# Key and value projections of a memory cross-attention: a third pair of k-tiles taken in seven products

## The chip, the cores and the metric

The kernel runs on one core of a Trainium2 chip. The metric is device time in microseconds (us) of one launch; the time of a version is the median of its runs. A core has a matrix engine (TensorE: PE in the profile, with its weight loads as PEld), three engines that work on tiles (VectorE: DVE, ScalarE: ACT, GpSimd: POOL), and a queue from which almost all transfers are issued (SP). Each engine takes its instructions in the order in which the program was built, and waits on semaphores for the results of the others.

## The reference

A streaming-encoder block of one layer over 256 tokens of width 2048, in float32: a gated feed-forward, a mixer, a cross-attention to 256 memory tokens, and a second feed-forward. What matters here is the cross-attention:

```python
def mem_cross_attention(h, mem_h, w_q, w_kv, w_o):
    b, s, _ = h.shape
    q = (h @ w_q).reshape(b, s, XATTN_HEADS, XATTN_HEAD_DIM)
    kv = (mem_h @ w_kv).reshape(b, mem_h.shape[1], 2, XATTN_HEADS, XATTN_HEAD_DIM)
    k, v = kv[:, :, 0], kv[:, :, 1]
    logits = jnp.einsum('bshd,bmhd->bhsm', q, k).astype(jnp.float32) * (XATTN_HEAD_DIM ** -0.5)
    p = jax.nn.softmax(logits, axis=-1).astype(v.dtype)
    o = jnp.einsum('bhsm,bmhd->bshd', p, v).reshape(b, s, D_MODEL)
    return o @ w_o
```

`w_kv` is 2048 x 4096: 16 k-tiles of 128 rows, and four blocks of 1024 columns, which are taken as keys of heads 0 and 1, values of heads 0 and 1, keys of heads 2 and 3, values of heads 2 and 3.

## The kernel before

**Precision by halves.** Every float32 operand is kept as a high and a low part in a faster format, and one product of tiles is three matmuls: high by high, high by low, low by high (`products`, L357). A weight tile arrives by a 1 MB transfer as `raw`; ScalarE casts the high part `wh` (L1579), VectorE subtracts to make the low part `wl` (`low_parts`, L453). `raw`, `wh` and `wl` have three buffers each.

**Units and the stream.** A block multiplies 256 tokens by 1024 columns. It is cut into eight units, one for each pair of k-tiles; the order of the units is a tuple such as `KV_ORDER`. `Stream.emit` (L70) writes the program out unit by unit: the weights of the unit two places ahead are split, the transfer three places further is issued, then the unit's matmuls follow. Side work is put among the units by `st.op(f, after)`. VectorE's and ScalarE's work on weights keeps its written order (`in_turn`, L257). The order of matmuls on TensorE is settled when the program is built, and neighbouring units can be interleaved by it.

**Two kinds of unit.** A plain unit (`unit_p`) is 2 k-tiles x 2 token halves x 2 column halves x 3 = 24 matmuls of 128 x 512. The other kind (`unit_s`, `seven`, L493) takes the 2 x 2 x 2 product of half blocks in seven products instead of eight, which is 7 x 3 = 21 matmuls, after the scheme of Strassen and Winograd. For that, sums of the operands are needed:

- of the weights, for each such unit and block: `split_seven` (L471) makes four sums in `T` with three VectorE instructions (L486), splits three of the raw parts into `xh` (ScalarE, L279) and `xl` (VectorE, L280), and the four sums into `wh` (ScalarE, two casts, L489) and `wl` (VectorE, L453);
- of the tokens, once for each pair of k-tiles: `Sums.make` (L413) makes them on VectorE in a scratch tile `j` and splits them into a tile `ye` and, for one of them, over the second half of the pair's own columns of `xs`, which holds the memory tokens here.

Partial results of the seven products lie in two extra PSUM tiles (`parts`), which `combine` (L570) adds up after the last such unit; `join` (L584) adds the result to the block's other two PSUM tiles. There are four PSUM tiles in all. The logits, the softmax and the products with the values run among the units of the following block, and use PSUM tiles too.

**Where the sums lie.** While the keys and values are made, `T` takes turns with the tile of `combine` in two buffers called `sg`, and `xh` and `xl` have together two buffers called `att`:

```python
    KV_HOMES = {"T": [("sg", D, 2)], "xh": [("att", 3 * NB, 2)], "xl": [("att", 3 * NB, 2)]}
```

So the `xh` and `xl` of one unit fill both, and those of the next unit of this kind go where these have been read for the last time. In the blocks of the queries `xh` and `xl` have other places besides (`Q_HOMES`, L1229).

**The blocks in question.** All four use the order (1, 5, 2, 0, 3, 6, 4, 7), with pairs 0 and 4 in seven products: the fourth and the seventh unit (L1288, L1374 to L1387). The sums of the tokens of these two pairs are made at the start of the first key block.

Of the kernel before, what the change touches and what calls it, by code (L numbers as in the profile page):

```python
# [20 lines left out]
NB = 512  # L21
# [78 lines left out]
def build(ctx, tc, I, out):  # L100
# [89 lines left out]
    xs = main.tile([P, KT, 2, S], F32R, tag="xs", name="xs")  # L190
# [79 lines left out]
    def among_weights(f):  # L270


        scalar, vector = behind_weights(f)
        latest["vector"] = vector
        if scalar is not None:
            latest["scalar"] = scalar
# [349 lines left out]
    def wload(dst, w, k0, n, n0, cols=NB):  # L626
        nc.sync.dma_start(
            dst, w[k0 * P : (k0 + n) * P, n0 : n0 + cols].rearrange("(k p) n -> p k n", p=P)
        )
# [9 lines left out]
    def wwide(w, n0, k0=0, nk=KT):  # L639

        def src(k):
            def load(raw):
                raw = raw.rearrange("p (k n) -> p k n", n=2 * NB)
                if len(loaded) < 3:
                    for kk in range(2):
                        parts = (0, NB) if not loaded else (0,)
                        for c in parts:
                            n = 2 * NB // len(parts)
                            wload(raw[:, kk : kk + 1, c : c + n], w, k + kk, 1, n0 + c, n)
                else:  # L650
                    wload(raw, w, k, 2, n0, 2 * NB)
                next(first_loads, None)
                loaded.append(1)
            return load
        return [src(k0 + k) for k in range(0, nk, 2)]
# [577 lines left out]
    def homes(of):  # L1233
        return lambda: scope.update(shared={tag: list(of[tag]) for tag in of})
# [47 lines left out]
    w_q, w_kv, w_o = I["xattn_w_q"][0], I["xattn_w_kv"][0], I["xattn_w_o"][0]  # L1282
# [2 lines left out]
    q_sums, Q_ORDER = Sums("ye", xs, (4, 5), True, 2), ((0, 1, 2, 3, 6, 4, 5, 7),  # L1285
                                                        (0, 1, 4, 2, 5, 3, 6, 7))
    Q_SEVENS = ((4,), (4, 5))
    kv_sums, KV_ORDER = Sums("ye", xs, (0, 4), True, 2), (1, 5, 2, 0, 3, 6, 4, 7)  # L1288
    held = {}

    def ev_Q(b):
# [10 lines left out]
    def turn_K(h):  # L1302
        v = rows_turned(held["K", h])
        K = xa["K", h] = xt("K", [P, 4, 2, M], F32R, tag="kv", bufs=2)
        split(K[:, :, 0, :], K[:, :, 1, :], v)

    def ev_V(b):
        def evict(j, c):
            V = xa["V", 2 * b + j] = xt("V", [P, 2, 2, XHD], F32R, tag="kv", bufs=2)
            split(V[:, :, 0, :], V[:, :, 1, :], c)  # L1310
        return evict

    def logits(h):
        ps = ptile(uid("pl"))
        for t in range(2):
            tok = slice(t * P, (t + 1) * P)
            parts = [(d, a, b) for d in range(4) for a, b in ((0, 0), (0, 1), (1, 0))]
            for i, (d, a, b) in enumerate(parts):
                nc.tensor.matmul(  # L1319
                    ps[:, t, :M], ys[:, 4 * h + d, a, tok], xa["K", h][:, d, b, :],  # L1320
                    start=i == 0, stop=i == 11,
                )
        scale = XHD ** -0.5
        nm, sm = xt("nm", [P, 2], bufs=2), xt("sm", [P, 2], bufs=2)
        nc.vector.tensor_reduce(out=nm, in_=ps[:, :, :M], axis=AX.X, op=ALU.max)
        nc.vector.tensor_scalar_mul(nm, nm, -scale)
        pr = xa["P", h] = xt("P", [P, 2, M], bufs=2)
        for t in range(2):
            nc.scalar.activation(
                pr[:, t, :], ps[:, t, :M], AF.Exp, scale=scale, bias=nm[:, t : t + 1],  # L1330
                accum_out=sm[:, t : t + 1],
            )
        nc.vector.reciprocal(out=sm, in_=sm)
        for t in range(2):
            nc.vector.tensor_scalar_mul(pr[:, t, :], pr[:, t, :], sm[:, t : t + 1])

    def probs(h):
        ps = ptile(uid("pt"))
        for mtile in range(2):
            for t in range(2):  # L1340
                nc.tensor.transpose(
                    ps[:, mtile, t * P : (t + 1) * P], xa["P", h][:, t, mtile * P : (mtile + 1) * P], ident
                )
        if h % 2 == 0:
            xt("PT", [P, D], F32R)
        PT = xa["PT", h] = xa["PT"][:, h % 2 * 4 * S : (h % 2 + 1) * 4 * S].rearrange(
            "p (m a s) -> p m a s", m=2, a=2
        )
        split(PT[:, :, 0, :], PT[:, :, 1, :], ps[:, :, :S])

    def values(h):
        for p in range(2):
            ps = ptile(uid("pv"))
            for d in range(2):
                col = slice((2 * p + d) * P, (2 * p + d + 1) * P)
                parts = [(m, a, b) for m in range(2) for a, b in ((0, 0), (0, 1), (1, 0))]
                for i, (m, a, b) in enumerate(parts):
                    nc.tensor.matmul(  # L1358
                        ps[:, d, :S], xa["V", h][:, m, a, col], xa["PT", h][:, m, b, :],
                        start=i == 0, stop=i == 5,  # L1360
                    )
            split_pair(ys, 4 * h + 2 * p, ps[:, :, :S])
# [8 lines left out]
            for c, after in enumerate((5, 7, 6, 9)):  # L1371
                st.op(lambda c=c: mem_fold(c), after)
    st.op(homes(KV_HOMES))
    for g, after in zip(kv_sums.pairs, (0, 2)):  # L1374
        st.op(lambda g=g: among_weights(lambda: kv_sums.make(g)), after)
    for b in range(2):
        block_s(wwide(w_kv, b * 2 * NB), xs, kv_sums, KV_ORDER, lambda j, c, b=b: held.__setitem__(
            ("K", 2 * b + j), c))
        for j in (1, 0):
            h = 2 * b + j  # L1380
            st.op(lambda h=h: turn_K(h), 1)
        for h in (2 * b, 2 * b + 1):
            st.op(lambda h=h: logits(h), 2)
            st.op(lambda h=h: probs(h), 3)
        block_s(wwide(w_kv, D + b * 2 * NB), xs, kv_sums, KV_ORDER, ev_V(b))
        for h in (2 * b, 2 * b + 1):
            st.op(lambda h=h: values(h), 1)  # L1387
# [211 lines left out]
def program(shapes):  # L1599
    import concourse.bacc as _bacc  # L1600

    nc = _bacc.Bacc("TRN2", target_bir_lowering=False, num_devices=1)
    args = {
        name: nc.dram_tensor(f"in_{name}", shapes[name], F32, kind="ExternalInput").ap()
        for name in _INS
    }
    out = nc.dram_tensor("out", _OUT, F32, kind="ExternalOutput").ap()
    with tile.TileContext(nc, schedule_with_timeline_sim=True) as tc, ExitStack() as ctx:
        build(ctx, tc, args, out)
    return nc  # L1610
# [10 lines left out]
```

## Time and profile before

| | us |
|---|---|
| median of three runs | 2083.23 (2082.67 to 2083.72) |
| the profiled execution, whole time | 2082.87 |
| the profiled execution, span from the first to the last instruction | 2081.1 |
| between the two | 1.8 |

The granted TensorE clock was 0.999 on average. The key and value blocks lie between about 1085 and 1289 us of the span; their 32 transfers of 1 MB took 5.0 us from issue to landing (median).

How to read the views: the page's first part gives busy time, share of the span and instructions of each engine; its groups give line, engine, operation, the tile written and the tiles read, count, busy time and the mean of one in ns, then the idle time of that engine just before. The timeline gives start and length in us, the instruction (consecutive ones of a kind are merged, with xN), and in square brackets the engine's idle time before it with what ended it. A matmul's length in these views is from its start to its modelled end; matmuls overlap, so the distance from one start to the next is what it takes of TensorE's time.

### The profile page before, as it was taken

Reading aid. Unit: us, or ns where it says so; the run is one execution under the profiler, and the core shown is the slowest. Engines: PE = TensorE matmul, PEld = TensorE weight load, DVE = VectorE, ACT = ScalarE, POOL = GpSimd, SP = SyncE. Lnnn points to the kernel's source line nnn. Section 1 sums busy time; section 2 is a strip of 40 time slices with the busy share of each in tenths; the row PEclk is TensorE's granted clock in tenths of the full one; section 3 lists DMA queues with packets and bytes.
Section 4 is the critical chain, followed back from the end, with each engine's and each line's share of the span. In section 5 each row is a group of like instructions: output and inputs, shape, how many; then the busy total and the mean of one; then the engine's idle time right before and its main releaser. Section 6 shows DMA issues by size and latency. Waiting matters only on the chain.

```text
span 2081.1 us, 24343 instructions
## 1 busy us (share of the span) xinstructions
PE 2069.6 (99%) x9660; PEld 1727.6 (83%) x9660; DVE 1786.6 (86%) x1670; ACT 1138.7 (55%) x1128; POOL 98.4 (5%) x87
## 2 busy tenths in 40 slices
PE   9999999999999999999999999999999999999998
PEld 7888888888888888888888888888888888888886
DVE  7998899989998677679788777879988999889987
ACT  7655455644654545455755444656554555545554
POOL 0000000000000000000000000000100010000001
PEclk9999999999999999999999999999999999999999
DMA  7666666566656755557655455666576665676664
GB/s 264 207 201 227 235 223 219 185 223 239 227 199 218 249 167 182 162 185 272 226 179 190 162 182 180 205 222 203 181 242 212 237 207 193 223 242 222 210 226 151
DMA packets 131178, 435.95 MB, mean 209 GB/s; under 512 B 9844, under 2 KB 13528, under 8 KB 130680
## 3 DMA queue, kind: packets, MB, share of 16 engines
q1 hardware_dynamic: 130888, 433.86, 61.9%
q8 instruction: 76, 1.25, 0.2%
q10 hardware_dynamic: 176, 0.53, 0.1%
q14 instruction: 38, 0.31, 0.0%
HBM read 417.58 MB, written 16.78 MB: 209 GB/s over the span
## 4 chain that ended last, share of the span: by engine, by line
PE 99%; DMA 0%; DVE 0%; ACT 0%; SPq 0%; DVEq 0%; issue 0%; ACTq 0%
PE pt L362 59%; PE pt L507 27%; PE pa L347 7%; PE pb L362 2%; PE ph L780 1%; PE pl L1319 1%; PE pv L1358 1%; PE px L791 1%; PE pp L1012 0%; PE pe L362 0%; DMA x<-in_x 0%; PE pa L1039 0%; PE po L1161 0%; PE tm L1267 0%; PE px L717 0%; PE pq L1148 0%
## 5 line engine op out<-in xcount | busy, mean ns | idle before, releaser
L362 PE MATMUL pt<-wh,xs 128*128 128x512 f32 x2128 | 682.4, 390 | 0.1
L453 DVE TENSOR_TENSOR wl<-raw,wh 128x2048 fp32r<-128x2048 f32 (+1 forms) x256 | 552.1, 2162 | 141.7 <-ACT wh L1579 141.3
L1579 ACT CAST wh<-raw 128x2048 fp32r<-128x2048 f32 x256 | 489.4, 1913 | 300.7 <-PE pt L362 134.5
L362 PEld LDWEIGHTS pt<-wh,xs 128*128 128x128 f32 x2128 | 398.7, 188 | 81.9 <-ACT xs L236 0.4
L362 PE MATMUL pt<-wh,ys 128*128 128x512 f32 x1472 | 463.9, 389 | 0.0
L489 ACT CAST wh<-T 128x1024 fp32r<-128x1024 f32 x236 | 248.1, 1055 | 366.7 <-DVE T L486 355.8
L362 PE MATMUL pt<-wl,xs 128*128 128x512 f32 x1064 | 414.5, 390 | 0.0
L362 PEld LDWEIGHTS pt<-wh,ys 128*128 128x128 f32 x1472 | 276.2, 188 | 56.9
L362 PE MATMUL pt<-wl,ys 128*128 128x512 f32 x736 | 286.8, 390 | 0.0
L453 DVE TENSOR_TENSOR wl<-T,wh 128x2048 fp32r<-128x2048 f32 (+1 forms) x118 | 264.7, 2243 | 0.8 <-ACT wh L489 0.4
L362 PEld LDWEIGHTS pt<-wl,xs 128*128 128x128 f32 x1064 | 199.8, 188 | 41.0
L280 DVE TENSOR_TENSOR xl<-raw,xh 128x1536 fp32r<-128x1536 f32 x118 | 206.7, 1751 | 18.9 <-ACT xh L279 18.9
L279 ACT CAST xh<-raw 128x1536 fp32r<-128x1536 f32 x118 | 174.6, 1480 | 44.0 <-PE pt L507 35.1
L486 DVE TENSOR_TENSOR T<-T,raw 128x512 f32<-128x512 f32 x236 | 162.9, 690 | 6.2
L362 PEld LDWEIGHTS pt<-wl,ys 128*128 128x128 f32 x736 | 138.2, 188 | 28.6
L486 DVE TENSOR_TENSOR T<-raw 128x1024 f32<-128x1024 f32 x118 | 143.8, 1218 | 0.5
L507 PE MATMUL pt<-wh,xs 128*128 128x512 f32 x364 | 141.8, 390 | 0.0
L457 POOL TENSOR_TENSOR wl<-raw,wh 128x768 fp32r<-128x768 f32 x40 | 74.1, 1852 | 1376.2 <-DVE wl L453 1339.2
L507 PE MATMUL pt<-xh,xs 128*128 128x512 f32 x364 | 135.8, 389 | 0.0
L347 PE MATMUL pa<-xs,wh 128*128 128x512 f32 x384 | 135.6, 397 | 0.0
L507 PE MATMUL pt<-wh,xe 128*128 128x512 f32 x320 | 124.3, 389 | 0.0
L347 PE MATMUL pa<-xs,wl 128*128 128x256 f32 x384 | 106.8, 282 | 0.0
(248 smaller groups left out, 2312.4 us busy)
## 6 DMA issues: line engine op xcount, KB each, us to landing
raw<-in_ffn_w_down SPq DMA_DIRECT2D x88, 1024.0 KB, 5.6
raw<-in_ffn_w_up SPq DMA_DIRECT2D x80, 1024.0 KB, 5.0
raw<-in_ffn_w_gate SPq DMA_DIRECT2D x77, 1024.0 KB, 5.1
raw<-in_w_in SPq DMA_DIRECT2D x32, 1024.0 KB, 5.3
raw<-in_xattn_w_kv SPq DMA_DIRECT2D x32, 1024.0 KB, 5.0
raw<-in_w_out SPq DMA_DIRECT2D x16, 1024.0 KB, 5.6
raw<-in_xattn_w_q SPq DMA_DIRECT2D x16, 1024.0 KB, 5.6
raw<-in_xattn_w_o SPq DMA_DIRECT2D x16, 1024.0 KB, 5.6
```

The lines of the kernel that those rows point to most:

```text
L279: in_turn("scalar", lambda: nc.scalar.copy(hi, src))
L280: in_turn("vector", lambda: nc.vector.tensor_tensor(out=lo, in0=src, in1=f32(hi), op=ALU.subtract))
L347: nc.tensor.matmul(o, w, x, start=k == 0 and i == 0, stop=last and i == 1)
L362: nc.tensor.matmul(ps, a, w, start=first and i == 0, stop=last and i == 2)
L453: in_turn("vector", lambda: nc.vector.tensor_tensor(out=lo[:, :n], in0=src[:, :n], in1=f32(hi[:, :n]), op=ALU.subtract))
L457: rest = nc.gpsimd.tensor_tensor(out=lo[:, n:], in0=src[:, n:], in1=f32(hi[:, n:]), op=ALU.subtract)
L486: in_turn("vector", lambda: nc.vector.tensor_tensor(out=o, in0=a, in1=b, op=ALU.add))
L489: in_turn("scalar", lambda: nc.scalar.copy(th[:, c], t[:, c]))
L507: nc.tensor.matmul(banks[n], x, w, start=n in fresh and j == 0, stop=n in ends and j == 2)
L780: nc.tensor.transpose(v[:, i, h * P : (h + 1) * P], g[:, h, i * P : (i + 1) * P], ident)
L791: nc.tensor.transpose(v[:, j, h * P : (h + 1) * P], x[:, h, j * P : (j + 1) * P], ident)
L1579: in_turn("scalar", lambda: nc.scalar.copy(hi, raw))
```

## The change

In three of the four blocks (values of heads 0 and 1, keys and values of heads 2 and 3) pair 2 is taken in seven products as well, and the order of the units becomes (1, 5, 3, 0, 6, 4, 2, 7): seven products in fourth, sixth and seventh place. The first key block keeps its order and its two pairs. The sums of the tokens of pair 2 are made during the first key block, after its fifth unit; the third unit has read pair 2 in the plain form by then. The tile `ye` grows from two parts to three.

```diff
-    kv_sums, KV_ORDER = Sums("ye", xs, (0, 4), True, 2), (1, 5, 2, 0, 3, 6, 4, 7)
+    kv_sums = Sums("ye", xs, (0, 4, 2), True, 3)
+    KEY_ORDER, KV_ORDER = (1, 5, 2, 0, 3, 6, 4, 7), (1, 5, 3, 0, 6, 4, 2, 7)
     held = {}
...
-    for g, after in zip(kv_sums.pairs, (0, 2)):
+    for g, after in zip(kv_sums.pairs, (0, 2, 5)):
         st.op(lambda g=g: among_weights(lambda: kv_sums.make(g)), after)
     for b in range(2):
-        block_s(wwide(w_kv, b * 2 * NB), xs, kv_sums, KV_ORDER, lambda j, c, b=b: held.__setitem__(
-            ("K", 2 * b + j), c))
+        block_s(wwide(w_kv, b * 2 * NB), xs, kv_sums, KV_ORDER if b else KEY_ORDER,
+                lambda j, c, b=b: held.__setitem__(("K", 2 * b + j), c),
+                sevens=() if b else (0, 4))
```

In `block_s`, `sevens=()` means all pairs of the sums.

In the program as built, TensorE has 9 matmuls of 128 x 512 fewer, and the three blocks show one and the same pattern. The products of the first unit of this kind that need `parts` (three on `xh` and `xl`, then nine on `wh` and `wl`) stand behind the plain unit that follows it, as before. Behind them stand now the two other units of this kind, 21 matmuls each. Within each of the two, with the places counted from 0: three on `xh`, one on `wh` (place 3), the first on `xl` (place 4), up to the last on `xh` (place 9), and then those on `wh` and `wl`. The first on `wl` has place 12 in the earlier one and place 13 in the later one, where one matmul of the last plain unit stands in front of it. VectorE's order there is `xl`, `wl` of the earlier unit, then the three sums into `T`, `xl` and `wl` of the later one, then `wl` of the plain unit. ScalarE's is `xh`, `wh` (two casts) of the earlier, `xh`, `wh` (two casts) of the later, then `wh` of the plain unit.

## The prediction

> **What bounds the kernel now.** I read the page's first part, then the windows of the key and value blocks, then the timelines of TensorE, ScalarE and VectorE in one of them (values of heads 0 and 1).
>
> ```profile
> span 2081.1 us, 24343 instructions
> PE 2069.6 (99%) x9660; PEld 1727.6 (83%) x9660; DVE 1786.6 (86%) x1670; ACT 1138.7 (55%) x1128; POOL 98.4 (5%) x87
> PE 99%; DMA 0%; DVE 0%; ACT 0%; SPq 0%; DVEq 0%; issue 0%; ACTq 0%
> L362 PE MATMUL pt<-wh,xs 128*128 128x512 f32 x2128 | 682.4, 390 | 0.1
> ```
>
> ```profile
> core 0: us, PE busy (x) PEld busy (x) DVE busy (x) ACT busy (x) POOL busy (x), PEclk, DMA share, GB/s
> 1109.00:1141.00 32.00, 32.00 (x146) 26.57 (x145) 26.68 (x25) 16.15 (x13) 3.70 (x2) 1.00 0.60 200
> 1141.00:1191.00 50.00, 50.00 (x254) 42.49 (x253) 35.59 (x35) 26.14 (x28) 3.72 (x2) 1.00 0.49 165
> 1191.00:1240.00 49.00, 49.00 (x245) 41.63 (x244) 35.23 (x30) 21.79 (x18) 3.71 (x2) 1.00 0.54 176
> 1240.00:1289.00 49.00, 49.00 (x248) 41.62 (x247) 34.97 (x38) 23.59 (x27) 3.71 (x2) 1.00 0.53 182
> ```
>
> The chain that ended last is TensorE alone, and TensorE is full in all four blocks; VectorE is busy some 71% of the last three (35.59 of 50.00). But a matmul's mean of 390 ns overlaps with the next one's, so "busy" hides short waits. What a matmul costs, and whether TensorE waits, is read from the starts:
>
> ```profile
> 1169.44 0.39 PE L507 MATMUL pt<-xh,xs 128*128 128x512 f32 x1
> 1169.67 0.39 PE L507 MATMUL pt<-xl,xs 128*128 128x512 f32 x1
> ...
> 1171.93 0.39 PE L507 MATMUL pt<-wh,ye 128*128 128x512 f32 x1
> ...
> 1175.33 0.62 PE L507 MATMUL pt<-xh,xs 128*128 128x512 f32 x2
> ...
> 1176.24 0.39 PE L507 MATMUL pt<-xl,xs 128*128 128x512 f32 x1
> ...
> 1178.28 0.39 PE L507 MATMUL pt<-wl,xs 128*128 128x512 f32 x1
> ```
>
> From 1169.44 to 1175.33 stand 26 matmuls, 0.227 us each, and no gap. Twelve of them are the first seven-product unit's (1169.44 to 1171.93), 14 belong to the plain unit; at 1175.33 the second unit of this kind begins, its first product on `xl` at 1176.24, on `wl` at 1178.28. The other engines' side of the same stretch:
>
> ```profile
> 1170.09 1.48 ACT L279 CAST xh<-raw 128x1536 fp32r<-128x1536 f32 x1 [5.79 <-PE pt L507]
> 1171.48 2.00 ACT L489 CAST wh<-T 128x1024 fp32r<-128x1024 f32 x2
> ```
>
> ```profile
> 1171.61 1.76 DVE L280 TENSOR_TENSOR xl<-raw,xh 128x1536 fp32r<-128x1536 f32 x1 [4.23 <-ACT xh L279]
> 1173.51 2.29 DVE L453 TENSOR_TENSOR wl<-T,wh 128x2048 fp32r<-128x2048 f32 x1
> 1175.72 3.68 DVE L453 TENSOR_TENSOR wl<-raw,wh 128x2048 fp32r<-128x2048 f32 x2
> ```
>
> The second unit's `xh` can't be cast before the first unit's `xh` and `xl` have been read, because both pairs share the two `att` buffers: the cast starts at 1170.09, 0.65 after the first reader started at 1169.44, and ends ScalarE's idle time of 5.79. `xl` is ready at 1171.61 + 1.76 = 1173.37, 2.9 us before it is read. That margin comes from the plain unit's matmuls in between.
>
> **The change part by part.** *Saved:* three units lose 3 matmuls each, 9 x 0.227 = 2.04 us, all on the path. The Trainium skill, "TensorE: Matmul & The Clock Gate" (Wait — 56ns, not 53.3ns?), puts the distance of such matmuls at 215.7 ns; by that estimate the saving would be 1.94 and the sum below 0.1 us higher. The trace's 0.227 decides.
>
> *Work added beside it.* Each new unit costs VectorE three sums and an `xl` more (4.4 us: 2.59 and 1.75, rows below), and ScalarE some 1.6 us (a cast of 1.48 and two of 1.0 in place of one long one). The new token sums are bounded by those of the second pair:
>
> ```profile
> core 0: us, DVE busy (x) ACT busy (x), PEclk, DMA share, GB/s
> 1106.00:1117.00 11.00, 2.60 (x7) 0.70 (x2) 1.00 0.52 184
> ```
>
> ```profile
> 1126.80 1.49 DVE L453 TENSOR_TENSOR wl<-raw,wh 128x1280 fp32r<-128x1280 f32 x1 [2.85 <-ACT wh L1579]
> ```
>
> They fall into the first key block, where VectorE idles 2.85 us at a stretch just after; I cost their 2.60 at nothing, and without that cover at most 2.6 once. In total VectorE gets some 3 x 4.4 + 2.6 = 15.8 us on top of 132.5 in 180, so it isn't short on the whole. Transfers, their number and queue stay as they are.
>
> *The wait.* In the three blocks the plain unit's place is taken: behind the twelve products comes at once the sixth unit (21 products), then the seventh (21), both in seven products, and one pair of `att` buffers serves three units in a row. I count from the start of the first reader (0; here 1169.44). TensorE without waits would be at places 16 (first `xl` of the sixth unit), 24 (`wl`), 37 (`xl` of the seventh), 46 (`wl`), times 0.227: 3.63, 5.45, 8.40, 10.44. What they need is a chain through ScalarE and VectorE, whose steps the rows above have, plus the sums into `T`, which VectorE's order puts behind the sixth unit's `wl`:
>
> ```profile
> 1117.80 1.75 DVE L280 TENSOR_TENSOR xl<-raw,xh 128x1536 fp32r<-128x1536 f32 x1
> 1119.47 2.29 DVE L453 TENSOR_TENSOR wl<-T,wh 128x2048 fp32r<-128x2048 f32 x1
> 1121.67 2.29 DVE L453 TENSOR_TENSOR wl<-raw,wh 128x2048 fp32r<-128x2048 f32 x1
> ...
> 1139.17 1.22 DVE L486 TENSOR_TENSOR T<-raw 128x1024 f32<-128x1024 f32 x1
> ...
> 1141.76 1.75 DVE L280 TENSOR_TENSOR xl<-raw,xh 128x1536 fp32r<-128x1536 f32 x1
> ```
>
> So sums to `xl` take 2.59, `xl` to `wl` 1.67, one `wl` to the next 2.20. What a late part costs TensorE, the trace shows in the query blocks, where two such units stand one plain unit apart:
>
> ```profile
> 1066.14 0.39 PE L507 MATMUL pt<-wh,xs 128*128 128x512 f32 x1
> 1066.49 0.50 PE L507 MATMUL pt<-xl,xs 128*128 128x512 f32 x1
> 1066.83 0.39 PE L507 MATMUL pt<-xh,xs 128*128 128x512 f32 x1
> ```
>
> ```profile
> 1064.68 1.76 DVE L280 TENSOR_TENSOR xl<-raw,xh 128x1536 fp32r<-128x1536 f32 x1 [4.33 <-ACT xh L279]
> ```
>
> `xl` ends at 1066.44, its reader starts 0.05 later instead of 0.227 after the matmul before it, and the next one comes after 0.34 instead of 0.227: a wait costs 0.11 on top. Now the chain:
>
> - Sixth unit's `xl`: starts at 2.17 (1171.61), ends at 3.93, reader at 3.98 instead of 3.63. Late by 0.35, with the 0.11 by 0.46.
> - Its `wl`: starts at 4.07 (1173.51, held by the casts of `wh` to 1173.48), ends at 6.36, reader at 6.41 instead of 5.45 + 0.46 = 5.91: 0.50 and 0.11 more, late by 1.07.
> - Seventh unit's `xl`: VectorE is free at 6.28 (1175.72), the sums take 2.59, so it starts at 8.87, ends at 10.62; reader at 10.67 instead of 8.40 + 1.07 = 9.47: 1.20 and 0.11 more, late by 2.38. (`xh` isn't what holds it: its buffer is read for the last time at place 20, about 5.0, so its cast is over by 7.)
> - Its `wl`: starts at 10.54, ends at 12.83, reader at 12.88 instead of 12.82: 0.06 and 0.11, late by 2.55.
> - The last plain unit's `wl`: ends at 10.54 + 2.20 + 2.29 = 15.03; its reader (place 56) is due at 15.26. No wait, with 0.2 to spare.
>
> Bounds: if the 0.11 came only in part, the chain on VectorE would still end where it does, 2.44; were each step of the chain 2% longer, 2.8. I take 2.55, 2.3 to 2.9 for the range. Three blocks: 7.65.
>
> *Sum.* 7.65 - 2.04 = 5.6 us more. The profiled execution took 2082.87 (span 2081.1 and 1.8 around it), so 2088.5; the runs' median stands 0.36 above it, so 2088.8.
>
> **The rivals.**
>
> *VectorE and ScalarE keep up.* TensorE saves 2.04 and waits for nothing: 2081.2, not slower. For it: VectorE is idle 29% of these blocks, and no gap shows in them now. Against it: the idle time can't be used, because each step waits for the one before, and the buffer for its reader. It decides only where the chain is 2.5 us shorter in each block.
>
> *The sums come early.* If VectorE made the seventh unit's sums in the 4.23 us that it idles before the sixth's `xl`, that unit's `xl` would start at about 7, be read in time, and only the first two waits would stay: 1.07 a block, 3 x 1.07 - 2.04 = +1.2, 2084.4. Against it: the written order has them behind `wl`.
>
> *The delay goes on into the next block.* VectorE adds up the partial results behind the chain:
>
> ```profile
> 1180.69 0.69 DVE L575 TENSOR_TENSOR sg<-pt,sg 128x512 f32<-128x512 f32 x1 [1.29 <-ACT sg L574]
> 1181.41 1.23 DVE L576 TENSOR_TENSOR sg<-pt,sg 128x1024 f32<-128x1024 f32 x1
> 1182.67 0.69 DVE L579 TENSOR_TENSOR sg<-pt,sg 128x512 f32<-128x512 f32 x1
> ```
>
> Only at its end (1183.36) are the PSUM tiles free that the next block opens with. By the chain above it would begin at 12.74 + 2.20 + 1.40 (the next `wl`: 1.49 less the 0.09 by which 2.29 and 2.20 differ) = 16.3, take 2.67 (1180.69 to 1183.36) and end at 19.0, while the next block is due at place 78, 17.7 + 2.55 = 20.3: 1.3 to spare. From there on each us late is a us lost; at one more in each block, 2091.8.
>
> *The clock gives way.* In the query blocks the waits above left the granted clock alone:
>
> ```profile
> 1064.00:1072.00 8.00, 7.93 (x34) 5.87 (x33) 7.12 (x4) 6.75 (x6) 0.00 (x0) 1.00 0.39 131
> ```
>
> If it were halved from the seventh unit's `xl` to place 56, 20 matmuls would take 0.227 more each, 4.5 a block: 2088.8 + 13.6 = 2102. "TensorE: Matmul & The Clock Gate" of the Trainium skill (A second HAM failure mode: psum-queue depth-cycling) reports frequent short idle times of TensorE that made its clock swing between half and full; the row just above doesn't bear it out here.
>
> **How the numbers follow.** Forecast 0.83 (its own range, with 2.3 to 2.9 a block, 2087.7 to 2089.9), keeping up 0.04, early sums 0.04, going on 0.07, clock 0.02. The range 2086.6 to 2090.6 takes in the forecast with some room and half of "going on", and leaves out the other cases and a little of the tails, under 2 in 10. 0.2% is 4.2 us, about what a measurement of this kernel can tell from no change: slower means above 2087.4, faster below 2079.1. Faster 0.01 (no case gets there; only something unseen), within 0.2% 0.11 (keeping up, early sums, and 0.03 of the forecast's lower tail), slower 0.88.
>
> **What would show it.** In the timeline of TensorE in each of the three blocks: starts 0.5 to 1.5 us apart in place of 0.227 at the first `xl` and `wl` of the sixth unit and the first `xl` of the seventh, the last of them the longest; none in the first key block. In VectorE's: `xl` of the seventh unit 2.6 us after the sums began, these right behind a `wl`. 9 matmuls fewer. Wrong it would be, if TensorE's starts stay 0.227 apart there, if the waits sit at the start of a block, or if the granted clock falls under 1.00.

## The result, and the profile after

The changed kernel takes 2088.9 us (median of 9 runs, 2088.35 to 2090.19), the kernel before 2083.43 beside it (9 runs, 2082.67 to 2083.93): 5.47 us more, ratio 1.0028 with a 95% interval of 1.0017 to 1.0038. It is slower, by 0.28%: the interval leaves out 1, though its lower end lies under the 0.2% that the prediction takes for the least that can be told from no change.

The page of the changed kernel, its span, its busy times, and the chain that ended last by engine and by line:

```profile
span 2087.8 us, 24351 instructions
PE 2071.2 (99%) x9651; PEld 1725.3 (83%) x9651; DVE 1800.5 (86%) x1689; ACT 1145.3 (55%) x1136; POOL 98.7 (5%) x87
PE 97%; DVE 1%; ACT 0%; DMA 0%; issue 0%; SPq 0%; DVEq 0%; ACTq 0%
PE pt L362 58%; PE pt L507 26%; PE pa L347 6%; PE pb L362 2%; PE ph L780 1%; PE pl L1320 1%; PE pv L1359 1%; PE px L791 1%; DVE wl L453 0%; DVE xl L280 0%; DMA x<-in_x 0%; PE pp L1012 0%; DVE T L486 0%; PE pe L362 0%; ACT xh L279 0%; ACT wh L489 0%
```

There are nine matmuls fewer (9651), yet TensorE's part of the chain falls from 99% to 97%, and what comes in has the names of the weight split: `wl`, `xl`, `T`, `xh`. "Busy" itself is no help: it rose by 1.6 us while work was taken out. In part that is the drawing: a matmul that waited is drawn 0.50 us long instead of 0.39, and one ahead of a wait is no longer overlapped by the next (rows below).

Where the time went is read from two matmuls which stand outside the changed stretch in both programs: the first transpose of the first key block and the first product of the output weights. In the changed kernel, then in the one before (start, length, instruction):

```profile
1141.16 1.91 PE L780 MATMUL ph<-ident,sg 128*128 128x128 f32 x16
...
1290.84 0.39 PE L362 MATMUL pt<-wh,ys 128*128 128x512 f32 x1
```

```profile
1140.26 1.91 PE L780 MATMUL ph<-ident,sg 128*128 128x128 f32 x16
...
1284.21 0.39 PE L362 MATMUL pt<-wh,ys 128*128 128x512 f32 x1
```

Between them lie 149.68 us, where there were 143.95: 5.73 more in these two executions, against 5.47 between the medians of the runs. The 0.90 by which the stretch begins later belongs to this one execution; it stands in the query blocks already, where nothing was changed (the `xl` of 1064.68 starts at 1065.57 here).

The three blocks by windows (busy time and count of each engine, granted clock as PEclk):

```profile
core 0: us, PE busy (x) PEld busy (x) DVE busy (x) ACT busy (x) POOL busy (x), PEclk, DMA share, GB/s
1141.00:1192.00 51.00, 49.51 (x250) 40.95 (x249) 38.32 (x39) 26.48 (x29) 3.72 (x2) 1.00 0.46 146
1192.00:1243.00 51.00, 49.53 (x238) 40.71 (x237) 39.41 (x33) 24.98 (x21) 3.72 (x2) 1.00 0.52 171
1243.00:1294.00 51.00, 49.49 (x249) 40.93 (x248) 38.38 (x39) 22.69 (x26) 3.71 (x2) 1.00 0.49 168
```

TensorE was full in each of them before; now it idles some 1.5 us in each, and the clock is at 1.00. VectorE is busy 75 to 77%, so there is still no shortage. Where TensorE stands still, its timeline shows in the block of the values of heads 0 and 1 (in brackets the idle time that the profile counts, and what ended it):

```profile
1168.06 0.39 PE L507 MATMUL pt<-xh,xs 128*128 128x512 f32 x1
...
1171.46 0.39 PE L507 MATMUL pt<-wh,xs 128*128 128x512 f32 x1
1172.04 0.50 PE L507 MATMUL pt<-xl,xs 128*128 128x512 f32 x1 [0.19 <-DVE xl L280]
1172.38 0.40 PE L507 MATMUL pt<-xh,xs 128*128 128x512 f32 x1
...
1173.78 0.40 PE L507 MATMUL pt<-wh,xs 128*128 128x512 f32 x1
1174.46 0.50 PE L507 MATMUL pt<-wl,xs 128*128 128x512 f32 x1 [0.29 <-DVE wl L453]
1174.80 0.39 PE L507 MATMUL pt<-wh,xs 128*128 128x512 f32 x1
...
1177.32 0.39 PE L507 MATMUL pt<-wh,xs 128*128 128x512 f32 x1
1178.72 0.50 PE L507 MATMUL pt<-xl,xs 128*128 128x512 f32 x1 [1.01 <-DVE xl L280]
...
1180.69 0.39 PE L362 MATMUL pt<-wh,xs 128*128 128x512 f32 x1
1180.92 0.49 PE L507 MATMUL pt<-wl,xs 128*128 128x512 f32 x1
1181.25 0.40 PE L507 MATMUL pt<-wh,xs 128*128 128x512 f32 x1
...
1183.31 0.39 PE L362 MATMUL pt<-wl,xs 128*128 128x512 f32 x1
```

Read from start to start: 0.58 to the first `xl`, 0.68 to the first `wl` of the sixth unit, 1.40 to the first `xl` of the seventh, where 0.227 is normal. What is over 0.227 (0.35, 0.45, 1.17) is 0.16 more than the idle time in brackets, because the matmul before is drawn 0.39 long, 0.16 longer than it takes of TensorE's time. The other two blocks have the same three rows, at 1221.92, 1224.34 and 1228.60 and at 1274.51, 1276.94 and 1281.19. VectorE's side, and one row of ScalarE's:

```profile
1170.22 1.76 DVE L280 TENSOR_TENSOR xl<-raw,xh 128x1536 fp32r<-128x1536 f32 x1 [4.09 <-ACT xh L279]
1172.11 2.29 DVE L453 TENSOR_TENSOR wl<-T,wh 128x2048 fp32r<-128x2048 f32 x1
1174.32 1.22 DVE L486 TENSOR_TENSOR T<-raw 128x1024 f32<-128x1024 f32 x1
1175.58 1.42 DVE L486 TENSOR_TENSOR T<-T,raw 128x512 f32<-128x512 f32 x2
1176.91 1.75 DVE L280 TENSOR_TENSOR xl<-raw,xh 128x1536 fp32r<-128x1536 f32 x1
1178.58 2.28 DVE L453 TENSOR_TENSOR wl<-T,wh 128x2048 fp32r<-128x2048 f32 x1
...
1184.39 0.68 DVE L575 TENSOR_TENSOR sg<-pt,sg 128x512 f32<-128x512 f32 x1
...
1186.36 0.69 DVE L579 TENSOR_TENSOR sg<-pt,sg 128x512 f32<-128x512 f32 x1
```

```profile
1173.52 1.49 ACT L279 CAST xh<-raw 128x1536 fp32r<-128x1536 f32 x1 [1.44 <-PE pt L507]
```

After idling 4.09 us VectorE works almost without a pause, and TensorE's gaps end 0.05 to 0.06 after its instructions do: 1170.22 + 1.76 = 1171.98 against 1172.04, 1176.91 + 1.75 = 1178.66 against 1178.72. The seventh unit's `xh` is ready at 1175.01, 1.9 before its `xl` begins. So it isn't `xh` that is late, but VectorE, and the sums are among what it does in between.

### The profile page after: what moved, and what is told of

It is laid out like the page before. It is cut to its first block, busy times and chain, and to the rows that moved or that the text cites. A ratio compares the mean times of both kernels' runs of the same rounds, so it can differ in the third digit from the quotient of the medians.

```text
span 2087.8 us, 24351 instructions
## 1 busy us (share of the span) xinstructions
PE 2071.2 (99%) x9651; PEld 1725.3 (83%) x9651; DVE 1800.5 (86%) x1689; ACT 1145.3 (55%) x1136; POOL 98.7 (5%) x87
## 4 chain that ended last, share of the span: by engine, by line
PE 97%; DVE 1%; ACT 0%; DMA 0%; issue 0%; SPq 0%; DVEq 0%; ACTq 0%
PE pt L362 58%; PE pt L507 26%; PE pa L347 6%; PE pb L362 2%; PE ph L780 1%; PE pl L1320 1%; PE pv L1359 1%; PE px L791 1%; DVE wl L453 0%; DVE xl L280 0%; DMA x<-in_x 0%; PE pp L1012 0%; DVE T L486 0%; PE pe L362 0%; ACT xh L279 0%; ACT wh L489 0%
## 5 line engine op out<-in xcount | busy, mean ns | idle before, releaser
L362 PE MATMUL pt<-wh,xs 128*128 128x512 f32 x2080 | 667.6, 390 | 0.0
L453 DVE TENSOR_TENSOR wl<-raw,wh 128x2048 fp32r<-128x2048 f32 (+1 forms) x253 | 545.0, 2160 | 129.1 <-ACT wh L1581 128.7
L1581 ACT CAST wh<-raw 128x2048 fp32r<-128x2048 f32 x253 | 483.4, 1913 | 291.4 <-PE pt L362 121.0
L362 PEld LDWEIGHTS pt<-wh,xs 128*128 128x128 f32 x2080 | 389.7, 188 | 80.2 <-ACT wh L1581 0.2
L489 ACT CAST wh<-T 128x1024 fp32r<-128x1024 f32 x242 | 254.3, 1054 | 364.6 <-DVE T L486 359.8
L362 PE MATMUL pt<-wl,xs 128*128 128x512 f32 x1040 | 405.1, 390 | 0.0
L453 DVE TENSOR_TENSOR wl<-T,wh 128x2048 fp32r<-128x2048 f32 (+1 forms) x121 | 271.5, 2243 | 0.8 <-ACT wh L489 0.4
L362 PEld LDWEIGHTS pt<-wl,xs 128*128 128x128 f32 x1040 | 195.4, 188 | 39.8
L280 DVE TENSOR_TENSOR xl<-raw,xh 128x1536 fp32r<-128x1536 f32 x121 | 211.8, 1751 | 17.1 <-ACT xh L279 17.1
L279 ACT CAST xh<-raw 128x1536 fp32r<-128x1536 f32 x121 | 179.2, 1481 | 45.7 <-PE pt L507 30.7
L507 PE MATMUL pt<-wh,xs 128*128 128x512 f32 x376 | 146.4, 389 | 0.0
```

What stands on the lines that cost most here:

```text
L279: in_turn("scalar", lambda: nc.scalar.copy(hi, src))
L280: in_turn("vector", lambda: nc.vector.tensor_tensor(out=lo, in0=src, in1=f32(hi), op=ALU.subtract))
L362: nc.tensor.matmul(ps, a, w, start=first and i == 0, stop=last and i == 2)
L453: in_turn("vector", lambda: nc.vector.tensor_tensor(out=lo[:, :n], in0=src[:, :n], in1=f32(hi[:, :n]), op=ALU.subtract))
L489: in_turn("scalar", lambda: nc.scalar.copy(th[:, c], t[:, c]))
L507: nc.tensor.matmul(banks[n], x, w, start=n in fresh and j == 0, stop=n in ends and j == 2)
```

## The experiments

Each has its times beside runs of the kernel before on the same chip (medians 2083.2 to 2083.4). All change the changed kernel unless said otherwise.

**1. The sums made early.** The three sums into `T` of the seventh unit move ahead of the sixth unit's `xl`, into VectorE's idle time.

```diff
+        t = made.pop(u) if u in made else weight_sums(u, raw)
+        if scope["shared"] is KV_NOW.get("homes") and st.units[u + 1][1] is split_seven:
+            made[u + 1] = weight_sums(u + 1, raws[u + 1])
...
         split_weights(rh, rl, raw[:, NB:])
...
```

> The changed kernel, but VectorE makes the seventh unit's three sums (into T) ahead of the sixth unit's xl instead of behind its wl; all work and all orders of units as in the changed kernel. Theory (a serial chain: shared att buffers, then xl, wl, sums, xl, wl): the seventh unit's xl then comes in time and only the sixth unit's two waits stay, 1.07 us a block, 3.2 in all, less 2.04 saved: before + 1.2 us (2084.6). Rival (VectorE has too much work in these blocks): the work is the same, so it stays at before + 5 to 6 (2089). Rival (the shared att buffers alone): the seventh unit's xh and xl still wait for the sixth's, so its wait of about 1.2 a block stays: before + 5.

Measured: 2085.01 (2084.33 to 2085.45), before 2083.22, ratio 1.0008 (0.9999 to 1.0017): 1.8 us more, where the changed kernel has 5.5. So 3.7 us of the loss are gone. VectorE and TensorE in the same block:

```profile
1174.87 1.76 DVE L280 TENSOR_TENSOR xl<-raw,xh 128x1536 fp32r<-128x1536 f32 x1 [0.60 <-ACT xh L279]
```

```profile
1174.32 0.50 PE L515 MATMUL pt<-wl,xs 128*128 128x512 f32 x1 [0.31 <-DVE wl L453]
```

Now `xl` of the seventh unit waits for `xh`, 0.60, and is done at 1176.63, before TensorE asks for it; in all three blocks the third gap is gone and the first two remain. By the two outside matmuls the stretch is 145.2 us (1141.01 to 1286.22), 1.3 more than before, where +1.2 had been worked out; the runs are 0.6 above that. The place of the sums in VectorE's order is thus shown to be the cause of the third gap.

**2. The last block alone.** The third pair in seven products only in the values of heads 2 and 3; the sums of its tokens are made during the third block.

```diff
+    KV_ORDERS = {(0, 0): ((1, 5, 2, 0, 3, 6, 4, 7), (0, 4)), (0, 1): ((1, 5, 2, 0, 3, 6, 4, 7), (0, 4)),
+                 (1, 0): ((1, 5, 2, 0, 3, 6, 4, 7), (0, 4)), (1, 1): ((1, 5, 3, 0, 6, 4, 2, 7), ())}
...
-    for g, after in zip(kv_sums.pairs, (0, 2, 5)):
+    for g, after in zip(kv_sums.pairs, (0, 2, 21)):
...
```

> The third pair only in the last of the four blocks (values of heads 2 and 3); the other three as before; the token sums of pair 2 are made in the third block. Theory: one block's waits, 2.55, less 0.68 saved: before + 1.9 us, with TensorE's gaps in the last block alone. Rival (a cost once for all, such as the larger tile or the token sums): before + 4 to 5. Rival (VectorE's load over the whole stretch): a third of the load fits easily, before - 0.7.

Measured: 2085.27, ratio 1.0011 (1.0002 to 1.002), 2.05 us more. The three gaps appear in that block alone, the longest at 1276.24 with the same idle time of 1.01. So the loss is that of a block, three times over, and doesn't hang on the blocks before it.

**3. A plain unit between any two.** The same 9 matmuls are saved and the same sums are made, but the seven-product units take second, fourth and sixth place.

```diff
-    KEY_ORDER, KV_ORDER = (1, 5, 2, 0, 3, 6, 4, 7), (1, 5, 3, 0, 6, 4, 2, 7)
+    KEY_ORDER = (1, 5, 2, 0, 3, 6, 4, 7)
+    KV_ORDERS = {(0, 1): (1, 0, 5, 4, 3, 2, 6, 7), (1, 0): (1, 0, 5, 4, 3, 2, 6, 7), (1, 1): (1, 0, 5, 4, 3, 2, 6, 7)}
...
```

> The changed kernel with the three seven-product units in second, fourth and sixth place of the three blocks, one plain unit between any two; the same sums, the same matmuls. Theory: the chain has a plain unit's 5.4 us more between two of them; small waits of 0.3 and 0.15 at xl and wl stay in two of the blocks: before + 0 to 0.8 us. Rival (VectorE's load): unchanged, before + 5 to 6.

Measured: 2083.9, ratio 1.0003 (0.9994 to 1.0012), 0.7 more, not to be told from no change. TensorE's starts still come 0.1 to 0.35 us late in places, most of them in the first two of the three blocks, some 1.8 us in all where the changed kernel loses 7.8; that is about what the nine matmuls save, so no gain is left. The work added on VectorE and ScalarE is the same as in the changed kernel, so it is the places that cost, not the work.

**4. Another place for one `xh`.** In the keys of heads 2 and 3 the sixth unit's `xh` gets a buffer of its own (`PT`, idle there), so that it need not wait for the fourth unit's readers.

```diff
+    K1_HOMES = {"T": [("sg", D, 2)], "xl": [("att", 3 * NB, 2)],
+                "xh": [("att", 3 * NB, 2), ("PT", D, 1), ("att", 3 * NB, 2)]}
...
+        if b:
+            st.op(homes(K1_HOMES))
...
```

> The changed kernel, but in the third block (keys of heads 2 and 3) alone the sixth unit's xh lies in a third place, the tile PT, which is free there; its cast needn't wait for the fourth unit's readers. VectorE's order and all work stay. Theory: in that block the chain starts earlier, the sixth unit's two waits go and the sums come sooner, so the seventh unit's xl is late by some 0.6 instead of 1.2; that block's 2.5 becomes about 0.8, the other two stay: before + 3.9 us (changed kernel - 1.8). Rival (only VectorE's order behind wl matters, the buffer doesn't): no change from the changed kernel, before + 5.6.

Measured: 2087.3, before 2083.4, ratio 1.002 (1.0011 to 1.0029): 3.9 more, where the changed kernel has 5.5. TensorE, then VectorE in that block:

```profile
1225.36 0.39 PE L507 MATMUL pt<-wh,xs 128*128 128x512 f32 x1
1226.19 0.50 PE L507 MATMUL pt<-xl,xs 128*128 128x512 f32 x1 [0.45 <-DVE xl L280]
```

```profile
1224.39 1.75 DVE L280 TENSOR_TENSOR xl<-raw,xh 128x1536 fp32r<-128x1536 f32 x1
```

The sixth unit's two gaps are gone, the seventh's is 0.83 - 0.227 = 0.60 (it was 1.2), and the other two blocks have theirs unchanged. So the two shared `att` buffers start the chain, and the sums lengthen it.

**5. Two units adjacent, nothing added.** The kernel before, with its two seven-product units in sixth and seventh place in three blocks.

```diff
+    LATER = (1, 5, 2, 3, 6, 0, 4, 7)
...
+        block_s(wwide(w_kv, b * 2 * NB), xs, kv_sums, LATER if b else KV_ORDER, lambda j, c, b=b: held.__setitem__(
...
+        block_s(wwide(w_kv, D + b * 2 * NB), xs, kv_sums, LATER, ev_V(b))
```

> The kernel before, without a third pair: pairs 0 and 4 only, but in the last three blocks in sixth and seventh place (order 1, 5, 2, 3, 6, 0, 4, 7) instead of fourth and seventh. No work is added and no matmul saved. Theory (neighbouring places with one pair of att buffers): waits of 2 to 2.3 us a block, before + 6 to 7 us. Rival (VectorE's load from the third pair): nothing added, before + 0.

Measured: 2090.22, ratio 1.0033 (1.0021 to 1.0046), 7.0 more, with the work of the kernel before. TensorE, then ScalarE, values of heads 0 and 1:

```profile
1177.06 0.73 PE L507 MATMUL pt<-xh,xs 128*128 128x512 f32 x2 [0.66 <-ACT xh L279]
...
1178.85 0.50 PE L507 MATMUL pt<-xl,xs 128*128 128x512 f32 x1 [0.35 <-DVE xl L280]
```

```profile
1175.53 1.48 ACT L279 CAST xh<-raw 128x1536 fp32r<-128x1536 f32 x1 [8.46 <-PE pt L507]
```

Here the sums were made long before. ScalarE idles 8.46 us until TensorE has read the buffers, and `xh` comes too late for the unit that follows at once. Adjacency alone makes a loss of this size.

**6. One sum made twice.** The first sum into `T` of the seventh unit is made a second time, in all three blocks: 1.22 us more on the chain.

```diff
+            if u in twice and o.shape[1] == 2:
+                in_turn("vector", lambda: nc.vector.tensor_tensor(out=o, in0=a, in1=b, op=ALU.add))
...
```

> The changed kernel, but the first of the three sums into T of the seventh unit (pair 2) is made twice in each of the three blocks: one more VectorE instruction of 1.22 us there, which changes no value. Theory (the sums lie in the chain that ends last): each lengthens the chain by 1.25, so before + 5.6 + 3.75 = before + 9.4 us, and the gap at the seventh unit's xl grows by as much. Rival (what holds the seventh unit is the att buffer or ScalarE, VectorE having time to spare, 29% idle): before + 5.6.

Measured: 2096.13 (5 runs), ratio 1.0062 (1.0049 to 1.0075): 12.7 more instead of 9.4. The waits of the seventh unit grew by as much as expected, though in two places: 0.66 at its first `wh` and 1.75 at its `xl`, 2.41 together, where there was 1.17 at `xl` alone. What was not expected stands behind them. Windows of this kernel (columns as above): the wait and the stretch behind it in the first and the second block, and the stretch in the third; then rows of TensorE from the first:

```profile
1176.00:1181.00 5.00, 3.02 (x13) 1.94 (x12) 4.90 (x6) 3.17 (x3) 0.00 (x0) 1.00 0.19 78
1181.00:1184.50 3.50, 3.50 (x11) 2.71 (x10) 3.50 (x2) 2.54 (x2) 0.00 (x0) 0.53 0.78 247
...
1229.00:1233.50 4.50, 2.54 (x11) 1.54 (x10) 4.43 (x5) 3.09 (x3) 0.00 (x0) 1.00 0.11 46
1233.50:1237.00 3.50, 3.50 (x16) 2.71 (x15) 3.50 (x2) 2.62 (x2) 0.00 (x0) 1.00 0.76 239
...
1287.00:1290.50 3.50, 3.50 (x8) 2.77 (x9) 3.50 (x2) 2.95 (x2) 0.00 (x0) 0.51 0.63 180
```

```profile
1177.70 0.39 PE L511 MATMUL pt<-xh,ye 128*128 128x512 f32 x1
1178.59 0.50 PE L511 MATMUL pt<-wh,xs 128*128 128x512 f32 x1 [0.50 <-ACT wh L493]
1180.57 0.50 PE L511 MATMUL pt<-xl,xs 128*128 128x512 f32 x1 [1.48 <-DVE xl L280]
...
1181.90 0.63 PE L511 MATMUL pt<-xl,ye 128*128 128x512 f32 x1
1182.33 0.63 PE L511 MATMUL pt<-xh,ye 128*128 128x512 f32 x1
```

From 1177.70 to 1180.57 a single matmul starts. Then the granted clock falls to half for some 3.4 us in the first and third block, matmuls come 0.43 apart, and in the second block it stays at 1.00. Some eight matmuls 0.20 dearer are 1.6 us, twice: 3.2, which with 9.4 makes 12.6. By the two outside matmuls the stretch is 12.3 longer than before. The chain theory holds, and the rival of the clock is real, one step beyond the changed kernel.

**7. The same sum three times, in one block.** Only in the keys of heads 2 and 3, the block that had kept its clock.

```diff
+            for _ in range(2 if u in thrice and o.shape[1] == 2 else 0):
+                in_turn("vector", lambda: nc.vector.tensor_tensor(out=o, in0=a, in1=b, op=ALU.add))
...
```

> Here the first of the three sums into T of the last seven-product unit is made three times, in the keys of heads 2 and 3 alone, of the three blocks the one in which the sum made twice had left the matmuls 0.227 us apart behind a wait of 1.7 us. Chain of waits alone: the two more sums make the chain there 2 x 1.23 = 2.46 us longer, all of it TensorE's; the time is the changed kernel's 2089.0 + 2.5 = 2091.4, the granted clock stays 1.00, the waits at the seventh unit's wh and xl are about 1.9 and 1.7. Clock gives way with the length of the waits: behind them some eight matmuls come 0.43 us apart, at a granted clock near 0.5, for 3.3 us, and the time is 2091.4 + 1.6 to 3.3 = 2093.0 to 2094.7.

Measured: 2093.33 (2092.64 to 2093.89), ratio 1.0048 (1.0035 to 1.006). Windows of that block:

```profile
1226.00:1230.50 4.50, 1.27 (x5) 0.53 (x4) 4.43 (x5) 3.02 (x3) 0.00 (x0) 1.00 0.00 0
1230.50:1234.00 3.50, 3.50 (x10) 2.68 (x10) 3.50 (x2) 2.67 (x2) 0.00 (x0) 0.51 0.75 241
```

With 3.23 us of 4.50 idle (4.50 - 1.27) the clock gives way in this block too, for 3.4 us. The waits by themselves would have ended at 2091.4; the eight dear matmuls make 2093.0.

**8. A version meant to be faster.** The third pair in two blocks only. The keys of heads 2 and 3 as in the changed kernel, with the edits of the first and fourth experiment; the values of heads 2 and 3 with the three units in second, fifth and sixth place.

```diff
+    KV_ORDERS = {(0, 0): ((1, 5, 2, 0, 3, 6, 4, 7), (0, 4)), (0, 1): ((1, 5, 2, 0, 3, 6, 4, 7), (0, 4)),
+                 (1, 0): ((1, 5, 3, 0, 6, 4, 2, 7), ()), (1, 1): ((1, 0, 5, 3, 4, 2, 6, 7), ())}
...
```

> The third pair in the last two blocks only. Third block: places as in the change, with the sums made early (as in e1) and the sixth unit's xh in PT (as in e4); last block: second, fifth and sixth place with the sums made early. Theory: with both links of the chain cut, TensorE waits for 0.2 us or so in all and keeps nearly all of 6 x 0.227 = 1.36 us: before - 1.0 us (2082.3). Rival (some wait always takes the saving back): before + 0 or more.

Measured: 2085.22 (2083.94 to 2085.8), before 2083.4, ratio 1.0008 (0.9999 to 1.0017): a miss by 2.8. ScalarE, VectorE and TensorE at the end of the last block:

```profile
1275.33 1.90 ACT L1597 CAST wh<-raw 128x2048 fp32r<-128x2048 f32 x1 [6.46 <-DMA raw<-in_xattn_w_o]
```

```profile
1277.27 1.49 DVE L453 TENSOR_TENSOR wl<-raw,wh 128x1280 fp32r<-128x1280 f32 x1 [5.32 <-ACT wh L1597]
1278.68 0.68 DVE L1337 TENSOR_REDUCE nm<-pl 128x2 f32<-128x512 f32 x1
```

```profile
1285.38 0.30 PE L1353 MATMUL pt<-ident,P 128*128 128x128 f32 x1 [2.05 <-DVE P L1347]
```

The softmax begins on VectorE with the maximum `nm`. It stands behind a `wl` of the output weights, which waits for a cast, which waits 6.46 us for its transfer; TensorE then waits 2.05 for the probabilities, which is most of the miss. With the weights' chain cut, something else became late that had not been so in the kernel before. Why this transfer lands later with these places was not followed.

**9. The same, with a plain unit between any two in the last block** (second, fourth and sixth place).

```diff
-                 (1, 1): ((1, 0, 5, 3, 4, 2, 6, 7), ())}
+                 (1, 1): ((1, 0, 5, 4, 3, 2, 6, 7), ())}
```

> The third pair in seven products in two blocks: keys of heads 2 and 3 in fourth, sixth and seventh place (sums into T made early, the sixth unit's xh in PT) as in the version with two blocks before, and values of heads 2 and 3 in second, fourth and sixth place, with a plain unit between any two. Chain of waits alone: 6 matmuls less save 1.36 us; in the keys 0.34, 0.03 and 0.15 us of waits stay, with 0.11 each 0.85 in all; none in the values: 0.5 us faster than before, 2082.9. Rival, the softmax of the last block stays late (its first instruction on VectorE stands behind a wl whose weights arrive late): the wait of 2.2 us at the transposes of the probabilities comes again, and the time is 2084.9 to 2085.2, as it was with the other places.

Measured: 2082.89 (2082.69 to 2084.28, 11 runs), before 2083.4 (15 runs), ratio 0.9998 (0.9989 to 1.0008). The median is where the sum had it, 0.5 below before, but the interval holds 1: no gain that these runs can show. The cast of the output weights waits for TensorE here, not for a transfer, and the wait at the transposes is gone. That the sum came out is in part luck. It had 0.85 us of waits left in the keys and none in the values; the trace has it the other way round. In the keys no start is late, and in the values the unit in fourth place has its first `xl` late by 0.35 (the row below, behind a start at 1251.00) and its first `wl` by 0.25, which with 0.11 behind each makes 0.82.

```profile
1251.58 0.50 PE L515 MATMUL pt<-xl,xs 128*128 128x512 f32 x1 [0.19 <-DVE xl L280]
```

## Why the prediction was right, step by step

It was 2088.8; the runs gave 2088.9. That the two agree to 0.1 is in part luck: the difference was put at 5.6 and is 5.47 by the runs and 5.73 by the profiled executions, and the kernel before, taken at 2083.23, has 2083.43 in the runs beside the changed one. The steps are the better test. The working counts from the start of the first reader, which is 1168.06 in the profile after:

| step | predicted | measured |
|---|---|---|
| sixth unit's `xl` read | 3.98 | 3.98 |
| its `wl` read | 6.41 | 6.40 |
| the sums begin | 6.28 | 6.26 |
| seventh unit's `xh` is ready | by 7 | 6.95 |
| seventh unit's `xl` begins | 8.87 | 8.85 |
| it is read | 10.67 | 10.66 |
| its `wl` read | 12.88 | 12.86 |
| place 56, how late (15.25 - 56 x 0.227) | 2.55 | 2.54 |
| the partial results are added up | 16.3 to 19.0 | 16.33 to 18.99 |

- *Saved* 2.04: nine matmuls fewer stand in the page. With 5.73 by the two outside matmuls, the three blocks lose 5.73 + 2.04 = 7.77, 2.59 each against the forecast's 2.55. The first key block has no gap, so the token sums made there did cost nothing.
- `xh` was ready when forecast, although its buffer is read for the last time at place 21 (1173.32, 5.26 after the first reader), not at place 20.
- *The 0.11 on top of a wait* came each time it was counted: 1172.38 - 1172.04 = 0.34, 1174.80 - 1174.46 = 0.34. It came also where the prediction had a wait of 0.06 before it, at the seventh unit's `wl`: that one shows no wait (1180.69 to 1180.92 is 0.23), but 1180.92 to 1181.25 is 0.33. The waits themselves were over by 0.14 in all: 0.35, 0.50, 1.20 and 0.06 in the working, 0.35, 0.45, 1.17 and none in the trace. Matmuls behind a wait make up for it, as they come 0.23 apart and a little more instead of 0.227 (six from 1172.38 to 1173.78 take 0.233 each). Up to the last wait the two had to cancel: a late product starts 0.05 to 0.06 after VectorE's instruction ends, so what the matmuls ahead of it lose comes off its wait, and VectorE's chain was forecast to 0.02.
- *Keeps up* falls: VectorE idles 23 to 25% of these blocks and TensorE waits for it. In the third experiment, with the same work, TensorE loses 1.8 us in place of 7.8.
- *The sums come early* is not what the program does, and its mechanism and price were right: made so in the first experiment, +1.3 in the stretch (+1.8 by the runs) against +1.2.
- *The delay goes on* falls: the partial results are added up at 18.99, and the next block opens without a gap.
- *The clock gives way* falls for this kernel, in which the clock is 1.00 throughout, as here in the middle block:

```profile
1227.00:1231.00 4.00, 3.01 (x13) 2.00 (x12) 4.00 (x3) 4.00 (x3) 0.00 (x0) 1.00 0.34 70
```

  It was nearer than 0.02 suggests: 1.22 us more on the chain brought it on in two of three places. Its price had been put at 4.5 a block, 20 matmuls; it was 1.6, 8 matmuls, because the half clock lasts some 3.4 us and not up to place 56.

## What to carry to other kernels

A unit with fewer products is only cheaper if its operands are ready. Where its preparation is a chain through two engines and a shared buffer, and the chain takes longer than the unit's own matmuls, the place in the order decides, and the idle shares of the engines on the chain (23 to 25% of VectorE here) don't show it. Count the places from the first reader to each need and put the chain's starts and ends beside them; here the loss of a block came out to a tenth of a microsecond that way. A plain unit between two of the dear kind is a cheap cover; sums that need only the raw data belong ahead of the wait, not behind it. Even so, no version here is shown to be faster than the kernel before: with a plain unit between, the waits left take back much of the saving (1.8 of 2.04 us in the third experiment, 0.82 of 1.36 in the ninth), and the rest is less than these runs can tell apart.

## What was not expected of the hardware

The granted clock fell to half behind waits in which TensorE wasn't wholly idle: in the sixth experiment's first block one matmul starts between 1177.70 and 1180.57, 2.87 us. Of the three waits of this kind in that kernel, each with one matmul in it, those of 2.87 and 2.90 (third block, 1284.10 to 1287.00) brought it on, and the one of 2.84 in the middle block (1230.30 to 1233.14) left the clock at 1.00. In the seventh experiment one of 4.12 (1226.09 to 1230.21, 3.23 us idle in 4.50) brought it on in that block too; the longest distance in the changed kernel's middle block, 1.38 from start to start (0.99 idle in 4.00), did not. Three waits that differ by 0.06 can't tell whether a limit of length lies between them or something else decides; that stays open.

The Trainium skill, "TensorE: Matmul & The Clock Gate" (What's actually happening), has a window of about 3.4 us that runs by itself, and the clock halves after an idle one. The length of the slow stretches agrees with that window (3.3 us from 1181.15 to 1184.46), and two like waits could fall differently into such windows; no run here moved a wait against them. That a whole window must be idle, these traces don't bear out: 2.87 us with a matmul in it was enough.
